# Moving the second feed-forward block's residual addition to VectorE, carrying Strassen-style sets into the last down projection, and adding ln3's beta through the output store

## The chip, the cores and the metric

The program runs on one NeuronCore of a Trainium2 chip. Its engines are TensorE (PE, matrix products), VectorE (DVE) and ScalarE (ACT) for elementwise work, GpSimd (POOL) for some elementwise work and for one kind of DMA, and SyncE (SP), which only issues DMAs here. The metric is device time of one execution in microseconds, lower is better. One execution also carries a hardware profile; its times of single instructions are what the text below quotes.

## The reference, cut to what matters

One decoder layer on 256 tokens of width 2048 in float32: a half-step feed-forward block, a mixer (windowed attention beside a convolution module), and a second half-step feed-forward block, each followed by a layer norm over alpha*x + block(x).

```python
def swiglu_ffn(x, w_gate, w_up, w_down):          # D_FF = 5632
    h = jax.nn.silu(x @ w_gate) * (x @ w_up)
    return h @ w_down
...
x = layer_norm(ALPHA * x + 0.5 * swiglu_ffn(x, ffn1...), ln1_g, ln1_b)
...                                                # mixer, then ln2
x = layer_norm(ALPHA * x + 0.5 * swiglu_ffn(x, ffn2...), ln3_g, ln3_b)
```

## The kernel before

**Products.** All large products keep float32 precision by splitting each operand into two parts, `hi` (rounded) and `lo` (the rest), and issuing three matmuls: hi*hi, hi*lo, lo*hi (`mm3`). One such product of a 128x128 block with 128x512 weights is three matmuls. For every weight tile of 128x1024, ScalarE makes `hi` by a cast and VectorE makes `lo` by a subtraction.

**Sets.** Where the two token blocks and two neighbouring k blocks meet two weight tiles, the code either issues the plain eight products (a set of kind "C", two weight sources) or a Strassen-Winograd form with seven (kind "S", four sources). An S set saves one product, three matmuls, and costs VectorE: four subtractions of 128x512 on the weights (`sub`, tiles `more` and `sum`) and more `lo` tiles, because four combinations of weights are split rather than two tiles. The token side needs sums of blocks too: `xs` for the up projections (made by `sums_of`), and extra slots of `hh` and `hl`, the split hidden activations, for the down projections.

**Parts.** A feed-forward block runs in three parts of the hidden width (16, 16 and 12 blocks of 128, `PARTS`). In a part, `pair` computes two groups of up and gate projections at a time from eight sets in the order of `UP`; the gated result is transposed (`turn`: VectorE transposes, POOL sends it through DRAM as `far` and back as `hf`), then split into `hh` and `hl` (`split`). Then the part's down projection runs. Parts 1 and 2 use `down_by_sums`: for each two of the four 512-wide column chunks, eight sets by `KINDS`; the results are added to a DRAM copy of the residual (`sides`) by accumulating DMAs. Part 3 has no kinds and uses `tokens_by`, which goes over single token blocks and column chunks, adds to the tokens in SBUF and feeds the layer norm's statistics.

**Queue of weights.** `Steps` holds the weight sources in order. Plain sources land in four `raw` tiles; the two weight tiles of an S set land in `more`, which lives in the same SBUF as the token tile `xt` (tag "xt", one buffer). So no S set can be loaded while `xt` is in use; `load` stops at the first S set until `placed` says that the place is free, and later sources wait behind it. In block two the place is free once `stored` holds all eight pieces, that is once the residual alpha*x has been scaled and written to DRAM (`residuals`, `y<-xt`). `tokens_back` takes the place back and reloads the tokens from DRAM (`xt<-y`); before, it is called in the last pair of part 3.

**Residual of block two.** `residuals(par2, 3, None, nc.vector, 1, 2)` runs beside the first token groups of block two (`token_group`: four groups of eight plain sources each). For each column chunk it loads the rows gain and beta, scales beta by alpha on ScalarE, scales the two token blocks on ScalarE, multiplies by the gain on VectorE (L592), adds beta, and stores (L611). The adding is an accumulating DMA on POOL's queue from SBUF to SBUF (L589, `xt<-rb`), and the store follows it in the same queue.

**Order.** Each engine runs its own list in order; the lists follow the order in which the Python code emits. Work is hung on coming steps by `st.at(delay, ...)`; while `st.paced` holds, `pace` puts a few VectorE jobs behind each product so that VectorE's planned backlog stays near `AHEAD`.

**End.** In `norm_to_rows` token block 0 is normalised while PE still runs the last eight half-steps of block 1 (`LAST`); gain and beta come by VectorE operations of the form (y - mean)*gain and y*r + beta (`scaled`, `last`), then plain stores on SP's queue. Block 1 follows after the last matmul.

Of the kernel before, what the change touches and what calls it, by code (L numbers as in the profile page):

```python
# [25 lines left out]
KINDS = ("SCCSCSCC", "SCCSCSCC", None)  # L26
BLOCKS = {"S": 7, "C": 4}
# [4 lines left out]
)  # L32
SUMMED = (0, 1)
# [42 lines left out]
def up_of(g, j0, plain):  # L76
    return 0 if g == plain else 2 if g == j0 // JG else 1

# [264 lines left out]
def hybrid_layer(  # L343
# [29 lines left out]
    def add_ffn(wu, wd, plain):  # L373
        for (j0, j1), kinds in zip(PARTS, KINDS):
# [94 lines left out]
    def row_chunk(r, c, name):  # L469
        t = act.tile([P, 512], F32, tag="bc", name=name, bufs=BC)  # L470
        nc.sync.dma_start(t, rows[r, c * 512 : (c + 1) * 512].partition_broadcast(P))
        return t
# [93 lines left out]
    def residuals(par, row, more, eng, start, every):  # L566
# [12 lines left out]
        for c in range(NC_):  # L579
            at = start + 1 + c * every  # L580

            def get(c=c, at=at):
# [36 lines left out]
    def norm_to_rows(b, stats, par, gb, store, kept):  # L619
# [24 lines left out]

        if b == 0:
            scaled(0)
            rsqrt(mv[:, 1:2], r, [lambda c=c: scaled(c) for c in range(1, NC_)])
        else:

            s = small.tile([P, 1], F32, tag="rs_v", name="rs_s")  # L650
            w = small.tile([P, 1], F32, tag="rs_w", name="rs_w")
            t = small.tile([P, 1], F32, tag="rs_t", name="rs_t")
            y = small.tile([P, 1], F32, tag="rs_y", name="rs_y")
            nc.scalar.activation(s, mv[:, 1:2], AF.Sqrt, bias=eps)
            nc.vector.tensor_scalar(out=w, in0=mv[:, 1:2], scalar1=EPS, scalar2=-0.5, op0=ALU.add, op1=ALU.mult)
            nc.vector.tensor_scalar(out=par[:, b, 3:4], in0=mv[:, 0:1], scalar1=-1.0, scalar2=None, op0=ALU.mult)
            nc.scalar.activation(ys[0], ys[0], AF.Identity, bias=par[:, b, 3:4])
            nc.vector.reciprocal(y, s)
            nc.gpsimd.tensor_scalar(out=t, in0=y, scalar1=y, scalar2=w, op0=ALU.mult, op1=ALU.mult)
            nc.gpsimd.tensor_scalar(out=r, in0=t, scalar1=1.5, scalar2=y, op0=ALU.add, op1=ALU.mult)  # L660
# [4 lines left out]
        if b == 0:  # L665
            for c in range(NC_):
                last(c)
        else:
# [11 lines left out]
    def block(x_, k, b):  # L680

        return x_[:, k, b * P : (b + 1) * P] if x_.shape[2] == S else x_[:, 2 * k + b]
# [117 lines left out]
    def tokens_by(lhs, k0, nk, factor, stats, finish, kept=None, lag=0):  # L800
# [7 lines left out]
        order = down_order(nk)  # L808
        skew = 0 if finish is None else SKEW if kept is None else LAST
        held, sums, halves = [], {}, []  # L810
        for n, (c, t) in enumerate(order):
            if t == 0:
                sums[c] = [psB.tile([P, 512], F32, tag="acc", name="acc0")]
                if kept is not None and c in (1, 2):
                    gu = psA.tile([P, 2, 512], F32, tag="gu", name="acc1")
                    sums[c].append(gu[:, 0])
                    halves.append(gu[:, 1, :256])
                else:
                    sums[c].append(psC.tile([P, 512], F32, tag="acc", name="acc1"))
                if kept is not None and c > 0:  # L820
# [6 lines left out]
            behind = lag if n < half - 1 else 0 if n < len(order) - skew else len(order)  # L827
# [89 lines left out]
    def down_by_sums(hh, hl, kinds, factor, side, more):  # L917

        firsts = [sum(BLOCKS[k] for k in kinds[:t]) for t in range(len(kinds))]
        places = {  # L920
            "S": ("11", "22", "12", "S1", "S2", "S3", "S4"),
# [7 lines left out]
        for c in range(0, NC_, 2):  # L929
# [6 lines left out]
            def shared(bank, tmp=tmp):  # L936
# [6 lines left out]
                add(tmp[3], bank[5], tmp[1])  # L943

            def leave(at, ps, c=c, tmp=tmp):
# [11 lines left out]
    def ffn(xc, tag, skew, begun, prepare, finish, places, back, kept=None):  # L957
        with tc.tile_pool(name=f"ffn{tag}", bufs=2) as pool:
# [4 lines left out]
            def sums_of(n):  # L963
# [10 lines left out]
                nc.vector.tensor_tensor(out=xs[:, n, 1], in0=part, in1=xs[:, n, 0].bitcast(F32), op=ALU.subtract)  # L974
# [17 lines left out]
            for part, ((j0, j1), kinds) in enumerate(zip(PARTS, KINDS)):  # L992
                n = j1 - j0
                ends = part == len(PARTS) - 1
                count = 2 * n if kinds is None else sum(BLOCKS[k] for k in kinds)
# [20 lines left out]
                def turn(g, ht, hh=hh, hl=hl, kinds=kinds):  # L1016
# [19 lines left out]
                    def split(hf, t):  # L1036
                        full = hf.rearrange("p (t k i) -> p k t i", t=4, k=8)
                        if kinds is None:
                            return parted(8 * g + 4 * t, full[:, 4 * t : 4 * t + 4])
                        kind = kinds[2 * g + t]  # L1040
                        at = sum(BLOCKS[k] for k in kinds[: 2 * g + t])
# [6 lines left out]
                        parted(at, some[:, 1:])  # L1048
                        parted(at + 3, sums)
# [3 lines left out]
                def pair(g, ups, last):  # L1053
# [7 lines left out]
                    def shared(bank):  # L1061
# [7 lines left out]
                        if last is not None:  # L1069
# [492 lines left out]
```

## Time and profile before

| | us |
|---|---|
| median of three runs | 1691.73 (1691.11 to 1694.22) |
| profiled execution | 1691.87 |
| its span on the core | 1690.1 |
| PE busy | 1666.7 |
| VectorE busy | 1392.0 |
| ScalarE busy | 925.8 |

The profiled execution is its span plus 1.8 us around it, and stands 0.14 us above the median. A page row names line, engine, operation, the tiles out<-in, the count, then busy time and the mean of one in ns, then idle time before it and what ended that. Matmul ends are modelled and overlap, so the rate of PE is read from counts over a stretch, not from the mean duration. The source lines of the three matmuls of a product are L676 to L678.

### The profile page before, as it was taken

To read this page: it belongs to the slowest core of one execution; us is meant where nothing else is said; L and a number is where in the kernel's file an instruction comes from. 1 tells how busy PE (TensorE), PEld (TensorE's weight loads), DVE (VectorE), ACT (ScalarE), POOL (GpSimd) and SP (SyncE) were. 2 spreads that over 40 slices of the span, in tenths; PEclk is the share of its full clock that TensorE was granted. 3 is DMA by queue.
4 is the path that set the end of the run, shared out by engine and by line. 5 is a ranking of instruction groups with operands and counts; after the bars stand their busy time and mean duration, and the time that the engine had idled before them with its cause. 6 is when DMAs were issued, how large, how long until landed. Compare 5 with 4: busy or idle time off the path is not lost.

```text
span 1690.1 us, 21889 instructions
## 1 busy us (share of the span) xinstructions
PE 1666.7 (99%) x7671; PEld 1383.4 (82%) x7671; DVE 1392.0 (82%) x2049; ACT 925.8 (55%) x1279; POOL 322.1 (19%) x298
## 2 busy tenths in 40 slices
PE   9999999999999999999999999799999999999997
PEld 7888888888888888888888888678888888888886
DVE  7899898888998877758887766699998888988767
ACT  6555555555555554576665564455555555555542
POOL 0100000111100010189997102000000000000100
PEclk9999999999999999999999999899999999999999
DMA  8667677677887667466654668666785666776683
GB/s 303 243 226 238 207 251 237 211 249 238 249 255 237 224 228 258 159 204 184 195 187 151 199 210 256 212 243 217 240 268 195 225 223 210 244 258 205 225 290 102
DMA packets 112239, 378.36 MB, mean 224 GB/s; under 512 B 14080, under 2 KB 14208, under 8 KB 112128
## 3 DMA queue, kind: packets, MB, share of 16 engines
q1 hardware_dynamic: 95760, 332.64, 56.7%
q0 software_dynamic: 16224, 44.05, 10.9%
q8 instruction: 60, 0.98, 0.2%
q14 instruction: 51, 0.42, 0.1%
q10 hardware_dynamic: 144, 0.26, 0.0%
HBM read 348.59 MB, written 26.21 MB: 222 GB/s over the span
## 4 chain that ended last, share of the span: by engine, by line
PE 90%; DVE 4%; DMA 4%; issue 1%; ACT 1%; POOL 0%; SPq 0%; DVEq 0%; ACTq 0%; POOLq 0%
PE sum L676 21%; PE sum L677 21%; PE sum L678 21%; PE acc L676 4%; PE acc L678 4%; PE acc L677 4%; DMA xt<-rb 2%; PE in_c L1213 2%; PE in_a L1213 2%; PE in_q L1213 1%; DVE lo L170 1%; PE grp L677 1%; PE grp L678 1%; PE grp L676 1%; PE in_a L1211 1%
## 5 line engine op out<-in xcount | busy, mean ns | idle before, releaser
L170 DVE TENSOR_TENSOR lo<-raw,hi 128x1024 fp32r<-128x1024 f32 x312 | 367.8, 1221 | 76.5 <-ACT hi L166 75.5
L676 PE MATMUL sum<-hi,xcat 128*128 128x512 f32 x1026 | 399.9, 390 | 9.3 <-DVE ht L1005 8.4
L677 PE MATMUL sum<-lo,xcat 128*128 128x512 f32 x1026 | 399.7, 390 | 1.4 <-DVE lo L170 1.4
L678 PE MATMUL sum<-hi,xcat 128*128 128x512 f32 x1026 | 399.4, 389 | 0.0
L166 ACT CAST hi<-raw 128x1024 fp32r<-128x1024 f32 x312 | 315.5, 1048 | 88.9 <-DMA raw<-in_wu 43.3
L166 ACT CAST hi<-more 128x1024 fp32r<-128x1024 f32 x186 | 168.8, 908 | 178.1 <-DVE more L184 143.4
L249 ACT CAST hi<-raw 128x1024 fp32r<-128x1024 f32 (+1 forms) x180 | 182.6, 1031 | 121.9 <-PE acc L678 57.4
L676 PEld LDWEIGHTS sum<-hi,xcat 128*128 128x128 f32 x1026 | 192.9, 188 | 50.4 <-DVE ht L1005 8.8
L677 PEld LDWEIGHTS sum<-lo,xcat 128*128 128x128 f32 x1026 | 192.9, 188 | 41.5 <-DVE lo L170 1.8
L678 PEld LDWEIGHTS sum<-hi,xcat 128*128 128x128 f32 x1026 | 192.9, 188 | 40.1
L170 DVE TENSOR_TENSOR lo<-more,hi 128x1024 fp32r<-128x1024 f32 x186 | 190.2, 1042 | 32.4 <-ACT hi L166 32.3
L252 POOL TENSOR_TENSOR lo<-raw,hi 128x1024 fp32r<-128x1024 f32 x73 | 175.5, 2424 | 114.7 <-ACT hi L249 107.7
L676 PE MATMUL sum<-hi,hh 128*128 128x512 f32 x488 | 190.1, 390 | 0.5 <-DVE part L933 0.4
L1024 POOL DMA_DIRECT2D far<-hr x88 | 49.4, 577 | 738.6 <-DVE hr L1019 738.5
L678 PE MATMUL sum<-hi,hl 128*128 128x512 f32 x488 | 189.9, 389 | 0.0
L677 PE MATMUL sum<-lo,hh 128*128 128x512 f32 x488 | 189.8, 389 | 0.0
L166 ACT CAST hi<-sum 128x512 fp32r<-128x512 f32 x124 | 77.2, 622 | 171.2 <-DVE sum L184 166.5
L252 DVE TENSOR_TENSOR lo<-raw,hi 128x1024 fp32r<-128x1024 f32 (+1 forms) x107 | 126.1, 1204 | 45.7 <-ACT hi L249 44.9
L1058 DVE TENSOR_TENSOR part<-sum,part 128x512 f32<-128x512 f32 x152 | 100.7, 687 | 23.4 <-PE sum L678 16.4
L676 PEld LDWEIGHTS sum<-hi,hh 128*128 128x128 f32 x488 | 91.6, 188 | 20.6 <-DVE part L933 1.1
L678 PEld LDWEIGHTS sum<-hi,hl 128*128 128x128 f32 x488 | 91.6, 188 | 19.1
L677 PEld LDWEIGHTS sum<-lo,hh 128*128 128x128 f32 x488 | 91.6, 188 | 18.8
(202 smaller groups left out, 2514.2 us busy)
## 6 DMA issues: line engine op xcount, KB each, us to landing
raw<-in_wu SPq DMA_DIRECT2D x272, 512.0 KB, 5.1
raw<-in_wd SPq DMA_DIRECT2D x128, 512.0 KB, 5.0
more<-in_wu SPq DMA_DIRECT2D x76, 512.0 KB, 7.0
raw<-in_win SPq DMA_DIRECT2D x52, 512.0 KB, 4.0
more<-in_wd SPq DMA_DIRECT2D x48, 512.0 KB, 7.4
raw<-in_wout SPq DMA_DIRECT2D x32, 512.0 KB, 3.7
far<-hr POOLq DMA_DIRECT2D x88, 128.0 KB, 2.7
hf<-far POOLq DMA_DIRECT2D x22, 512.0 KB, 3.7
```

Of the source, the lines that this page charges most:

```text
L166: self.nc.scalar.copy(hi, x_)
L170: self.nc.vector.tensor_tensor(out=lo, in0=x_, in1=hi.bitcast(F32), op=ALU.subtract)
L249: nc.scalar.copy(hi, raw)
L252: eng.tensor_tensor(out=lo, in0=raw, in1=hi.bitcast(F32), op=ALU.subtract)
L676: nc.tensor.matmul(ps, s_hi, m_hi, start=start, stop=False)
L677: nc.tensor.matmul(ps, s_hi, m_lo, start=False, stop=False)
L678: nc.tensor.matmul(ps, s_lo, m_hi, start=False, stop=stop)
L1024: nc.gpsimd.dma_start(far[:, :, t].rearrange("f r n -> r f n"), hr[32 * t : 32 * t + 32])
L1058: nc.vector.tensor_tensor(out=out, in0=ps, in1=other, op=ALU.add)
L1211: nc.tensor.matmul(ps[:, :S], w[1][:, n], x1[:, k, 0, :], start=False, stop=k == KT - 1)
L1213: nc.tensor.matmul(ps, w[0][:, n], x1[:, k], start=k == 0, stop=False)
```

## The change

Four things change. (1) In `residuals`, beta is added by VectorE, as an operation of 128x512 behind each gain multiplication. (2) Part 3 gets kinds, "SCCSCC". Its column chunks 0 and 1 are computed by `down_by_sums`, whose results stay in SBUF and are added to the tokens by VectorE (`joins`) at the second to fifth step of the `tokens_by` that follows for chunks 2 and 3. `tokens_back` moves from the last pair to the last S set of that down projection. In these columns an S set keeps eight blocks of `hh`/`hl` (kind "L"), since the plain products need the fourth one. (3) `UP[2]`, the order of the first pair of parts 2 and 3 in both blocks, has three S sets for two; their token sums are made in part 2's first pair. (4) At the end, block 0's beta is written to `out` ahead by a broadcast DMA from DRAM to DRAM, and its normalised rows are added by four accumulating stores on POOL's queue; ScalarE does the scaling by r and VectorE only the gain. The loads of ln3's gain and beta move from SP's queue to POOL's and ScalarE's, and from step 6 to step 1. The two last half-chunks of block 1 get PSUM tiles of their own.

```diff
-KINDS = ("SCCSCSCC", "SCCSCSCC", None)
-BLOCKS = {"S": 7, "C": 4}
+KINDS = ("SCCSCSCC", "SCCSCSCC", "SCCSCC")
+BLOCKS = {"S": 7, "C": 4, "L": 8}
 UP = (
...
-    ((0, "S"), (2, "C"), (3, "C"), (1, "S"), (4, "C"), (5, "C"), (6, "C"), (7, "C")),
+    ((0, "S"), (3, "C"), (1, "S"), (4, "C"), (5, "C"), (2, "S"), (6, "C"), (7, "C")),
 )
-SUMMED = (0, 1)
+SUMMED = (0, 1, 2)
...
-            if kinds is None:
-                sources.extend(wd[c, j0 // 4 + t // 2, t % 2] for c, t in down_order(j1 - j0))
-                continue
             for c in range(0, NC_, 2):
+                if c > 0 and j1 == JT:
+                    sources.extend(wd[c + i, t // 2, t % 2] for i in range(2) for t in range(j0 // 2, j1 // 2))
+                    continue
                 for t, kind in enumerate(kinds, j0 // 2):
...
                 def on(out, a, b_, op):
-                    if eng is nc.vector and op is ALU.add:
-                        return lambda: nc.gpsimd.dma_start(out, b_, accum_op=ALU.add)
-
                     def work():
                         eng.tensor_tensor(out=out, in0=a, in1=b_, op=op)
...
+        minus, root, w, t, y = (small.tile([P, 1], F32, tag=f"rs_{k}", name=f"rs_{k}") for k in "nvwty")
+        nc.scalar.activation(root, mv[:, 1:2], AF.Sqrt, bias=eps)
...
         if b == 0:
-            scaled(0)
-            rsqrt(mv[:, 1:2], r, [lambda c=c: scaled(c) for c in range(1, NC_)])
+            nc.gpsimd.tensor_scalar(out=minus, in0=minus, scalar1=r, scalar2=None, op0=ALU.mult)
+
+            def rest(c):
+                nc.vector.tensor_tensor(out=ys[c], in0=ys[c], in1=gb[c][0], op=ALU.mult)
+                nc.gpsimd.dma_start(out[:P, c * 512 : (c + 1) * 512], ys[c], accum_op=ALU.add)
+
+            for c in range(NC_):
+                nc.scalar.activation(ys[c], ys[c], AF.Identity, scale=r, bias=minus)
+                st.at(c + 2, lambda c=c: rest(c))
...
+        if k0 == 0:
+            order = [x_ for x_ in order if x_[0] > 1]
...
             def leave(at, ps, c=c, tmp=tmp):
 
                 t = tmp[places_[at]]
                 add(t, ps, t)
+                if columns < NC_:
+                    y = xts[0][:, 1 - at[0], (c + at[1]) * 512 : (c + at[1] + 1) * 512]
+                    joins[1 - at[0], at[1]] = lambda: nc.vector.tensor_tensor(out=y, in0=y, in1=t, op=ALU.add)
+                    return
...
                         begun()
+                        nc.gpsimd.dma_start(out[:P], rows[6].partition_broadcast(P))
                         group(1, token_group(xc, 0))
...
+                    if part == 1 and g == j0 // JG:
+                        for m in range(2, len(SUMMED)):
+                            st.at(4, lambda m=m: st.soon.append(lambda: sums_of(m)))
...
-                st.at(6, lambda: prepare(pool))
+                st.at(1, lambda: prepare(pool))
...
+                for c in range(2):
+                    for b in range(2):
+                        st.at(2 + c + 2 * b, lambda b=b, c=c: stats_of(b, c))
                 tokens_by((hh, hl), 0, n, 0.5, stats, lambda b: finish(b, stats), kept)
```

Counted over the whole program, PE issues 24 matmuls of 128x512 fewer (12 in each block), VectorE issues 16 of `lo<-raw` fewer, 24 of `lo<-more`, 16 of `lo<-sum` and 32 weight subtractions more. Three places show how the lists move.

On POOL, beside the first token groups of block two (rb is alpha*beta, y the DRAM copy, far and hf the transposed hidden block on its way through DRAM). Before:

```order
L1141 MEMSET eps 128x1
L589 DMA xt<-rb_0_9112 128x512 x2
L611 DMA y_138<-xt 128x512 x2
L589 DMA xt<-rb_1_9152 128x512
L1024 DMA far<-hr 32x4x256 x4
L1026 DMA hf<-far 128x1024
L589 DMA xt<-rb_1_9152 128x512
L611 DMA y_138<-xt 128x512 x2
L589 DMA xt<-rb_2_9195 128x512 x2
L611 DMA y_138<-xt 128x512 x2
L589 DMA xt<-rb_3_9244 128x512 x2
L611 DMA y_138<-xt 128x512 x2
```

After:

```order
L1176 MEMSET eps 128x1
L1113 DMA out<-in_rows 128x2048
L612 DMA y_138<-xt 128x512 x2
L1044 DMA far<-hr 32x4x256 x4
L1046 DMA hf<-far 128x1024
L612 DMA y_138<-xt 128x512 x6
```

The eight accumulating DMAs are gone, and the broadcast to `out` stands right behind the memset.

On VectorE, behind the last pair of part 3 in block two (hr is that pair's transposed result, hf its return from DRAM, hl the lower half of its split, raw a plain weight tile, more an S set's). Before:

```order
L1019 STREAM_TRANSPOSE hr<-ht 128x1024
L252 TENSOR_TENSOR lo_14219<-raw_14103,hi_14218 128x1024
L252 TENSOR_TENSOR lo_14225<-raw_14121,hi_14224 128x1024
L252 TENSOR_TENSOR lo_14243<-raw_14139,hi_14242 128x1024
L252 TENSOR_TENSOR lo_14261<-raw_14157,hi_14260 128x1024
L252 TENSOR_TENSOR lo_14279<-raw_14222,hi_14278 128x1024
L252 TENSOR_TENSOR lo_14299<-raw_14228,hi_14298 128x1024
L252 TENSOR_TENSOR lo_14335<-raw_14246,hi_14334 128x1024
L1033 TENSOR_TENSOR hl_13148<-hf,hh_13147 128x512 x2
```

After, the end of the same stretch:

```order
L174 TENSOR_TENSOR lo_14390<-more,hi_14389 128x1024
L174 TENSOR_TENSOR lo_14401<-more,hi_14400 128x512
L174 TENSOR_TENSOR lo_14415<-raw_14266,hi_14414 128x1024
L174 TENSOR_TENSOR lo_14429<-raw_14284,hi_14428 128x1024
L174 TENSOR_TENSOR lo_14447<-raw_14331,hi_14446 128x1024
L174 TENSOR_TENSOR lo_14462<-raw_14340,hi_14461 128x1024
L1053 TENSOR_TENSOR hl_13251<-hf,hh_13250 128x512 x2
L174 TENSOR_TENSOR lo_14487<-raw_14432,hi_14486 128x1024
L174 TENSOR_TENSOR lo_14490<-raw_14438,hi_14489 128x1024
L938 SCALAR_TENSOR_TENSOR part<-sum,part 128x512 x4
```

Seven plain `lo` stood between the transposition and hl before; now a whole S set (nine rows, of which the last two are shown) and four plain `lo` stand there, and the partial sums of the down's final S set follow.

On VectorE at the end, where token block 0 is normalised (par holds mean, variance and r, g and b are gain and beta, acc is a PSUM tile of token block 1). Before, the end of that work:

```order
L634 SCALAR_TENSOR_TENSOR xt<-xt,par_144,g_14330 128x512
L514 TENSOR_SCALAR rs_t<-par_144,rs_w 128x1
L515 TENSOR_SCALAR par_144<-rs_t,par_144 128x1
L640 SCALAR_TENSOR_TENSOR xt<-xt,par_144,b_14320 128x512
L640 SCALAR_TENSOR_TENSOR xt<-xt,par_144,b_14324 128x512
L640 SCALAR_TENSOR_TENSOR xt<-xt,par_144,b_14328 128x512
L640 SCALAR_TENSOR_TENSOR xt<-xt,par_144,b_14332 128x512
L488 SCALAR_TENSOR_TENSOR acc_14463<-acc_14463,xt 128x512
L494 BN_STATS st_14189<-acc_14463 128x6 x2
```

After, from the aggregated statistics of block 0 on:

```order
L625 BN_AGGR par_144<-st_14591 128x2
L648 TENSOR_SCALAR rs_w<-par_144 128x1
L649 TENSOR_SCALAR rs_n<-par_144 128x1
L652 RECIPROCAL rs_y<-rs_v 128x1
L659 TENSOR_TENSOR xt<-xt,g_14611 128x512
L492 SCALAR_TENSOR_TENSOR acc_14596<-acc_14596,xt 128x512
L498 BN_STATS st_14592<-acc_14596 128x6 x2
L659 TENSOR_TENSOR xt<-xt,g_14615 128x512
L659 TENSOR_TENSOR xt<-xt,g_14619 128x512
L659 TENSOR_TENSOR xt<-xt,g_14623 128x512
L492 SCALAR_TENSOR_TENSOR xt<-acc_14716,xt 128x512
```

Token block 1's next evacuation (L488, now L492) stood behind eight passes of 128x512 over block 0's tokens (four L634, of which the last is shown, and four L640); now it stands behind one (L659).

More of the change, by code (lines that the diff above doesn't have):

```diff
@@ L77, in up_of, with blocks_of @@
     return 0 if g == plain else 2 if g == j0 // JG else 1
+def blocks_of(columns):
+    return lambda kind: BLOCKS["L" if kind == "S" and columns < NC_ else kind]
 class Steps:
@@ L680, in block @@
     def block(x_, k, b):
-        return x_[:, k, b * P : (b + 1) * P] if x_.shape[2] == S else x_[:, 2 * k + b]
+        if x_.shape[2] == S:
+            return x_[:, k, b * P : (b + 1) * P]
+        kinds = KINDS[-1]
+        return x_[:, sum(4 if y == "C" else 8 for y in kinds[: k // 2]) + 2 * (k % 2) + b]
     def token_mm(ps, lhs, k0, t, nk, b, w):
@@ L813, in tokens_by @@
                 sums[c] = [psB.tile([P, 512], F32, tag="acc", name="acc0")]
[L814 to L820, printed above, removed]
+                if kept is not None and c == 2:
+                    halves.extend(psA.tile([P, 2, 512], F32, tag="gu", name="acc1")[:, 0, :256] for _ in range(2))
+                sums[c].append(psC.tile([P, 512], F32, tag="acc", name="acc1"))
+                if kept is not None:
                     kept[1, c] = [sums[c][1]] if c < NC_ - 1 else halves
@@ L826, in tokens_by @@
             held.append((c, t, w))
-            behind = lag if n < half - 1 else 0 if n < len(order) - skew else len(order)
+            behind = len(order) if n >= len(order) - skew else lag if n < half - 1 else 0
             while len(held) > behind:
@@ L915, in by_sums, with down_by_sums @@
                 st.step(0)
-    def down_by_sums(hh, hl, kinds, factor, side, more):
-        firsts = [sum(BLOCKS[k] for k in kinds[:t]) for t in range(len(kinds))]
+    joins = {}
+    def down_by_sums(hh, hl, kinds, factor, side, more, columns, last):
+        firsts = [sum(map(blocks_of(columns), kinds[:t])) for t in range(len(kinds))]
         places = {
-            "S": ("11", "22", "12", "S1", "S2", "S3", "S4"),
+            "S": ("21", "11", "22", "12", "S1", "S2", "S3", "S4")[-blocks_of(columns)("S"):],
             "C": ("21", "11", "22", "12"),
@@ L927, in blocks @@
             return hh[:, n], hl[:, n]
-        for c in range(0, NC_, 2):
+        for c in range(0, columns, 2):
             tmp, places_ = [], {(0, 0): 0, (0, 1): 2, (1, 0): 1, (1, 1): 3}
@@ L943, in shared @@
                 add(tmp[3], bank[5], tmp[1])
+                if last is not None:
+                    last()
             def leave(at, ps, c=c, tmp=tmp):
@@ L994, in ffn @@
                 ends = part == len(PARTS) - 1
-                count = 2 * n if kinds is None else sum(BLOCKS[k] for k in kinds)
+                columns = 2 if ends else NC_
+                count = sum(map(blocks_of(columns), kinds))
                 hh, hl = (pool.tile([P, count, P], F32R, tag=t, name=f"{t}{part}", bufs=1) for t in ("hh", "hl"))
@@ L1014, in group, with turn @@
                         turn(g // 2, gated.pop())
-                def turn(g, ht, hh=hh, hl=hl, kinds=kinds):
+                def turn(g, ht, hh=hh, hl=hl, kinds=kinds, ends=ends, of=blocks_of(columns)):
                     hr = pool.tile([P, 4, 2 * P], F32, tag="ht", name="hr")
@@ L1047, in split, with pair @@
                         block_sums(view, [some[:, k] for k in range(4)])
-                        parted(at, some[:, 1:])
-                        parted(at + 3, sums)
+                        n = of(kind) - 4
+                        parted(at, some[:, 4 - n :])
+                        parted(at + n, sums)
                     st.at(6, lambda: st.soon.extend([lambda t=t: split(hf, t) for t in range(2)]))
-                def pair(g, ups, last):
+                def pair(g, ups):
                     tmp, places = [], {(0, 0): 0, (0, 1): 2, (1, 0): 1, (1, 1): 3}
```

69 lines of the change are left out of this document (36 added, 33 removed).

## The prediction

> **What bounds the kernel now.** I read the page first, then PE's busy time in 50 us stretches, then what PE waited for, then the chain of waits.
>
> ```profile
> PE 1666.7 (99%) x7671; PEld 1383.4 (82%) x7671; DVE 1392.0 (82%) x2049; ACT 925.8 (55%) x1279; POOL 322.1 (19%) x298
> ...
> 1000.00:1050.00 50.00, 50.00 (x222) 41.43 (x221) 32.80 (x47) 26.57 (x36) 10.48 (x15) 1.00 0.84 265
> 1050.00:1100.00 50.00, 40.20 (x164) 32.32 (x163) 30.40 (x40) 20.58 (x27) 6.90 (x11) 0.90 0.65 216
> ...
> 1200.00:1600.00 400.00, 400.00 (x1766) 331.31 (x1766) 347.75 (x438) 214.74 (x267) 30.19 (x47) 1.00 0.69 230
> ...
> PE sum L676 <- DVE ht L1005: 8.4, 1, 8.4
> PE sum L677 <- DVE lo L170: 1.4, 1, 1.4
> ...
> PE acc L676 <- DVE st L494: 0.8, 1, 0.8
> ```
>
> In the stretches, the columns after the length are busy time and count of PE, weight loads, VectorE, ScalarE, POOL, then PE's granted clock, the DMA share and GB/s. PE is the bound: it is busy without a break nearly everywhere, at 400/1766 = 0.2265 us per matmul in the long steady stretch, which is the price of a matmul below. One stretch is different: from 1050 to 1100 PE issues 164 matmuls where its neighbour has 222, and the clock drops. The two longest waits of PE lie there. The chain of waits (start, length, what) says why:
>
> ```profile
> 1009.62 9.78 DMA xt<-rb
> ...
> 1033.07 7.75 DMA xt<-rb
> 1041.79 8.28 DMA xt<-rb
> ...
> 1054.27 4.30 DMA xt<-rb
> 1058.97 2.35 DMA y<-xt
> 1061.78 4.36 DMA more<-in_wu
> 1066.23 0.70 DVE sum L184
> ...
> POOL y L611 <- DMA xt<-rb: 27.2, 7, 6.9
> ```
>
> The residual's beta is added by accumulating DMAs, whose landings follow each other in the chain; each store waits for them on POOL's queue (27.2 us in seven waits), and only when the last store has landed, at 1061.3, may the first S set's weights (`more`) be loaded. VectorE gets them at 1066.2. The releaser named for the 8.4 us, ht, is only VectorE work queued behind that set.
>
> What the whole disturbance costs is read between two fixed points, the first matmul of block two's first pair and that of part 2's first pair:
>
> ```profile
> 1052.81 0.39 PE L676 MATMUL sum<-hi,xcat 128*128 128x512 f32 x1
> ...
> 1235.40 0.39 PE L676 MATMUL sum<-hi,xcat 128*128 128x512 f32 x1
> ```
>
> Between them lie two pairs of 2 S and 6 C sets (2*7 + 6*8 = 62 products) and two down passes of 3 S and 5 C (61 products), so 246 products or 738 matmuls, 167.2 us at 0.2265. It took 182.6. The loss is **15.4 us**: 9.8 in the two waits, the rest in a slow clock and in shorter gaps behind.
>
> ```profile
> 1070.00:1075.00 5.00, 2.76 (x7) 2.18 (x8) 4.29 (x6) 1.70 (x5) 0.79 (x2) 0.50 0.74 302
> 1075.00:1080.00 5.00, 5.00 (x16) 3.95 (x15) 4.61 (x6) 3.77 (x6) 1.99 (x4) 0.66 0.76 189
> ```
>
> Of the 7.76 us that PE was busy here, 23 matmuls are worth 5.2 at full rate, so the clock cost 2.6. [...]
>
> **The change part by part.**
>
> *Beta by VectorE.* This takes eight accumulating DMAs out of POOL's queue and puts eight additions on VectorE.
>
> ```profile
> L592 DVE TENSOR_TENSOR xt<-xt,rg 128x512 f32<-128x512 f32 x8 | 5.5, 688 | 7.3 <-ACT xt L602 7.3
> ...
> 1028.75 0.69 DVE L592 TENSOR_TENSOR xt<-xt,rg 128x512 f32<-128x512 f32 x1
> ...
> 1054.03 1.23 DVE L252 TENSOR_TENSOR lo<-raw,hi 128x1024 fp32r<-128x1024 f32 x1 [0.68 <-ACT hi L249]
> ...
> 1019.88 25.30 SPq L110 DMA_DIRECT2D raw<-in_wu  x9
> ...
> more<-in_wu SPq DMA_DIRECT2D x76, 512.0 KB, 7.0
> ...
> y<-xt POOLq DMA_DIRECT2D x8, 256.0 KB, 4.3
> ```
>
> The last gain multiplication ends at 1029.4. With eight additions of 0.69, 5.5 us at most, the last piece is ready by 1035, and with 0.6 to issue and 4.3 to land the place is free by 1040. SP comes to the S set's request only behind the nine plain requests, at 1045.2, so the place is no longer what is late; the weights land at 1052.2, and VectorE reaches them behind its last plain `lo`, at 1055.3. PE needs the set behind two C sets, 48 matmuls after 1052.81: at 1063.7. An S set is some 7.2 us of VectorE work (below), its first tile ready after three or four of them, so there are about 5 us to spare. The additions themselves lie beside PE work on a VectorE that is busy 32.8 of 50 us; without that cover they would cost 5.5. I take the whole 15.4; the bounds are 15.4 and, if half of it stays, 7.7. The broadcast of beta to `out`, 1 MB, has no row of its own kind; it is issued behind the memset, before the residual's stores, and no one waits for it before the end. I take nothing; had it to move like four of the 256 KB stores at 4.3 us one after another, it would load the DMA engines for 17 us, against a prefetch several tiles ahead.
>
> *Fewer products.* Parts 2 and 3 of both blocks start with a third S set: four products. Part 3's down has two S sets, once per block for the two columns: four products. 8*3 = 24 matmuls at 0.2265 are **5.4 us**, if PE stays the bound. That depends on VectorE:
>
> ```profile
> L170 DVE TENSOR_TENSOR lo<-more,hi 128x1024 fp32r<-128x1024 f32 x186 | 190.2, 1042 | 32.4 <-ACT hi L166 32.3
> ...
> L170 DVE TENSOR_TENSOR lo<-raw,hi 128x1024 fp32r<-128x1024 f32 x312 | 367.8, 1221 | 76.5 <-ACT hi L166 75.5
> ...
> L170 DVE TENSOR_TENSOR lo<-sum,hi 128x512 fp32r<-128x512 f32 x124 | 80.2, 688 | 0.0
> ...
> L184 DVE TENSOR_TENSOR sum<-more,sum 128x512 f32<-128x512 f32 x62 | 42.9, 692 | 2.1
> ...
> L184 DVE TENSOR_TENSOR sum<-more 128x512 f32<-128x512 f32 x62 | 41.9, 676 | 13.1 <-DMA more<-in_wu 11.2 <-DMA more<-in_wd 1.7
> ...
> 1021.20 0.68 DVE L969 TENSOR_TENSOR full<-xcat 128x512 f32<-128x512 f32 x1
> ...
> 1023.63 0.69 DVE L974 TENSOR_TENSOR xs<-sums,xs 128x512 fp32r<-128x512 f32 x1 [0.69 <-ACT xs L973]
> ...
> 1446.80:1488.00 41.20, 41.20 (x184) 34.12 (x183) 38.41 (x49) 23.00 (x28) 4.48 (x6) 1.00 0.74 232
> ...
> 1238.00:1280.00 42.00, 42.00 (x187) 34.80 (x186) 33.47 (x39) 20.42 (x26) 1.51 (x2) 1.00 0.77 245
> 1488.00:1530.00 42.00, 42.00 (x187) 34.80 (x186) 33.71 (x40) 19.80 (x24) 2.19 (x3) 1.00 0.77 248
> ```
>
> An S set costs VectorE three `lo` from `more` (3.13), two from `sum` (1.38) and four subtractions between 0.68 and 0.69 (2.74): 7.2 us. A C set costs 2*1.22 = 2.4. A third S set adds 4.8. The two first pairs (last two rows) have 33.5 and 33.7 us of VectorE work in 42; part 3's becomes 38.5 in 41.2, which a down pass of 3 S sets carries today without a gap (38.4 in 41.2). Part 2's also gets the third token sums, 2.4 us of work (3.1 with its wait, 1021.20 to 1024.32): 40.9 in 41.2. That is fuller than any stretch here. VectorE runs several weight tiles ahead of PE, so a few tenths are absorbed; below nothing is excluded.
>
> *Part 3's down pass* puts S sets where the split of the last pair must come in time. In the down pass of part 2 the same sequence reads:
>
> ```profile
> 1404.24 1.29 DVE L1058 TENSOR_TENSOR part<-sum,part 128x512 f32<-128x512 f32 x2 [1.89 <-PE sum L678]
> ...
> 1424.50 1.29 DVE L1033 TENSOR_TENSOR hl<-hf,hh 128x512 fp32r<-128x512 f32 x2
> ```
>
> From PE's end of the pair to that split are 20.3 us. In part 3 the first four kinds, S C C S, keep PE for 30 products, 20.4 us, and the split is needed then; today the order there leaves room. Two of the S operations that stand ahead of it in part 2 are plain `lo` now, about as long. So it arrives as it is needed, with 0 to 2 us of waiting in each block. Together with part 2's full pair I put **1.4 us** of new waits against the saving (0.7 per block; bounds 0 and about 6). The joins, eight additions and their statistics, replace evacuations of the same columns beside PE work.
>
> *The end.*
>
> ```profile
> 1669.56 0.26 DVE L624 BATCH_NORM_AGGREGATE par<-st 128x2 f32<-128x24 f32 x1
> ...
> 1676.90 0.69 DVE L488 SCALAR_TENSOR_TENSOR acc<-acc,xt 128x512 f32<-128x512 f32 x1
> ...
> DMA to landing us min/median/max: 5.3/7.6/10.4
> ```
>
> Block 1's evacuation stands behind 7.3 us of block 0's normalisation. Behind one gain pass it comes while PE still works, so PE's wait of 0.8 (the last tile pair has its own PSUM now) and a little behind it go: **1.0 us**. The accumulating stores cost what the last row shows for such DMAs into DRAM (line L951): up to 10.4. The last is ready about 8 us after 1669.6, so it lands by 1688, when the plain last store does too. Nothing lost, or a few tenths.
>
> The sum against the profiled execution: 1691.87 - 15.4 - 5.4 - 1.0 + 1.4 = **1671.5** us, and 0.14 less against the median, which I ignore.
>
> **The rivals.**
>
> *VectorE becomes the bound.* If in part 2's and 3's first pairs and in the short down pass VectorE's work and its waits on ScalarE no longer fit, the eight products bring nothing, and part 2's pairs may even lengthen by the token sums, up to 2.4 in each block. For it speaks 40.9 of 41.2; against it, that 38.4 of 41.2 runs without a gap. Time: 1691.87 - 15.4 - 1.0 = 1675.5, up to 1680.3.
>
> *The stall stays in part.* The place is free, but the weights behind nine plain requests, or VectorE with 5.5 us more in its list, are late. For it: ScalarE and VectorE already wait on the rows of gain and beta (7.3 in L592's row). Against: 5 us to spare, and the accumulating traffic is gone. Half of 15.4 left: 1679.
>
> *The accumulating stores end the kernel.* If the four run one after another from 1674 on at 10.4 each, the last lands at 1715.6 where the span now ends at 1690.1, and the time is 1671.5 + 1 + 25.5 = 1698, slower than before; from about 9 us each it loses. In the chain the SBUF additions did follow each other. Against: L951's stores come in groups of four and none took longer than 10.4, so they overlap, and the DMA engines are nearly idle at the end.
>
> **How the numbers follow.** The forecast gets 0.70 with a range of its own of 1668 to 1675, the first rival 0.17, the second 0.10, the third 0.03. The range 1667.5 to 1681 takes in the first two rivals. A change of 0.2%, 3.4 us, is about what can be told from none. All but the third lie far below it: faster 0.96, within 0.01, slower 0.03.
>
> **What would show it right or wrong.** In the changed profile: no wait of PE above 2 us near 1060 and a granted clock of 1.00 there; `more` requested near 1045; 1766 matmuls in 400 us as before; VectorE above 40 of 41 us in part 2's first pair with PE unbroken; a PE wait on hl of under 2 us in the short down pass; the last landing a plain store. A wait of several us in any of these places, or an `out` accumulate landing last, would make it wrong.

## The result, and the profile after

The changed kernel takes **1674.91 us** (median of 4 runs, 1672.95 to 1675.41) against 1692.15 (4 runs, 1691.11 to 1694.22): a ratio of 0.9894, with a 95% interval of 0.9877 to 0.9912. That is 17.2 us faster. The forecast was 1671.5, 3.4 us too low; the range of 1667.5 to 1681 holds the time. The first rival's 1675.5 is nearer to it than the forecast, so the time alone does not tell the two apart, and the traces have to. The profiled execution took 1675.41 us, its span 1673.6.

The first group below is the page's busy time; the second is PE's busy time by stretches (length, then busy time and count of PE, weight loads, VectorE, ScalarE and POOL, then granted clock, DMA share, GB/s); the third is all that PE waited for.

```profile
PE 1657.9 (99%) x7647; PEld 1375.4 (82%) x7647; DVE 1444.1 (86%) x2151; ACT 944.6 (56%) x1316; POOL 323.0 (19%) x302
```

```profile
258.70:299.90 41.20, 41.20 (x183) 34.13 (x182) 38.84 (x51) 22.20 (x28) 2.19 (x4) 1.00 0.70 235
1050.00:1100.00 50.00, 49.44 (x217) 40.28 (x216) 41.49 (x55) 25.88 (x36) 2.80 (x5) 1.00 0.59 213
1200.00:1600.00 400.00, 400.00 (x1766) 331.20 (x1766) 362.58 (x470) 222.00 (x281) 27.19 (x42) 1.00 0.67 225
1219.99:1261.20 41.21, 41.21 (x183) 34.15 (x182) 39.52 (x53) 22.47 (x29) 2.93 (x4) 1.00 0.72 230
```

```profile
PE idle L415 <- DVE ones L412: 1.2, 1, 1.2
PE acc L678 <- DVE lo L256: 1.1, 2, 0.9
PE sum L677 <- DVE part L938: 1.0, 2, 0.9
PE grp L780 <- ACT hi L253: 0.5, 1, 0.5
PE sum L677 <- DVE part L1077: 0.4, 1, 0.4
```

The stretch from 1050 to 1100, which held 164 matmuls at a clock of 0.90, now holds 217 at 1.00. The waits of 8.4 and 1.4 us are gone; none is above 0.9 any more, apart from the start. 24 matmuls fewer are executed (7647 for 7671), and they still run at 1766 in 400 us. VectorE is at 38.8 and 39.5 of 41.2 us in the first pair of part 2 (first and last row of the stretches), in the two blocks, and PE has no gap there.

Where the time went is best read between fixed points of PE's instructions. The stretches are those of the prediction, in us; the second column of "after" is the changed kernel run once more. "Last form" is the version found below, with the PSUM bank and the spread joins (two runs).

| stretch | before | after | after, again | last form |
|---|---|---|---|---|
| block one, part 2's down | 83.93 | 85.71 | 84.85 | 84.66, 84.27 |
| block one, part 3's down | 67.28 | 65.71 | 65.80 | 65.70, 65.70 |
| block two, first sum to part 2's first sum | 182.59 | 168.43 | 168.29 | 168.60, 167.49 |
| pairs of part 2, each block | 168.64 | 167.96 | 167.96 | 167.96, 167.96 |
| pairs of part 3, each block | 126.48 | 125.80 | 125.80 | 125.80, 125.80 (126.01 once, in block one) |
| block two, part 3's down to the last matmul | 66.37 | 65.62 | 66.02 | 63.95, 63.95 |
| last matmul's start to the span's end | 10.24 | 11.27 | 11.25 | 10.43, 10.65 |

From before to after that is +1.8, -1.6, -14.2, four times -0.7, -0.75 and +1.0, which is 16.4 of the 16.5 us between the two profiled executions. Two rows got longer, and the prediction had neither lengthening: a down pass of block one, and the end.

The end, on VectorE and POOL (start, length, instruction, idle time before it and its releaser). Before:

```profile
1681.91 1.40 DVE L634 SCALAR_TENSOR_TENSOR acc<-acc,par,g 128x512 f32<-128x512 f32 x2
1682.11 0.34 POOL L659 TENSOR_SCALAR rs_t<-rs_y,rs_w 128x1 f32<-128x1 f32 x1 [52.28 <-DVE rs_y L658]
1682.79 1.26 POOL L662 TENSOR_TENSOR xt<-xt,g 128x512 f32<-128x512 f32 x1
1683.22 1.40 DVE L640 SCALAR_TENSOR_TENSOR xt<-acc,par,b 128x512 f32<-128x512 f32 x2
```

After:

```profile
1664.39 0.73 DVE L635 SCALAR_TENSOR_TENSOR xt<-xt,par,g 128x512 f32<-128x512 f32 x1
1664.58 0.76 POOL L653 TENSOR_SCALAR rs_t<-rs_y,rs_w 128x1 f32<-128x1 f32 x1 [1.59 <-DVE rs_y L652]
1665.67 1.26 POOL L667 TENSOR_TENSOR xt<-xt,g 128x512 f32<-128x512 f32 x1
1665.74 1.73 DVE L641 SCALAR_TENSOR_TENSOR xt<-xt,par,b 128x512 f32<-128x512 f32 x1
1667.39 0.74 DVE L641 SCALAR_TENSOR_TENSOR xt<-acc,par,b 128x512 f32<-128x512 f32 x1
```

The same work is longer in two places. POOL's one-column step takes 0.76 us instead of 0.34, and VectorE's first multiply-add takes 1.73, where its neighbour takes 0.74. Both overlap an instruction of the other engine. What is new is where column 1 of token block 1 lies: its name is `acc` (PSUM) before and `xt` (SBUF) after, because a join now produces it.

### The profile page after: what moved, and what is told of

It reads as the page before. It is cut to its first block, busy times and chain, and to the rows that moved or that the text cites. A ratio compares the mean times of both kernels' runs of the same rounds, so it can differ in the third digit from the quotient of the medians.

```text
span 1673.6 us, 21985 instructions
## 1 busy us (share of the span) xinstructions
PE 1657.9 (99%) x7647; PEld 1375.4 (82%) x7647; DVE 1444.1 (86%) x2151; ACT 944.6 (56%) x1316; POOL 323.0 (19%) x302
## 5 line engine op out<-in xcount | busy, mean ns | idle before, releaser
L170 ACT CAST hi<-more 128x1024 fp32r<-128x1024 f32 (+1 forms) x210 | 190.6, 907 | 178.8 <-DVE more L188 158.7
L174 DVE TENSOR_TENSOR lo<-more,hi 128x1024 fp32r<-128x1024 f32 (+1 forms) x210 | 213.7, 1040 | 20.3 <-ACT hi L170 20.2
L677 PE MATMUL sum<-hi,hh 128*128 128x512 f32 x580 | 226.2, 390 | 1.3 <-DVE part L938 1.0
L678 PE MATMUL sum<-lo,hh 128*128 128x512 f32 x580 | 225.7, 389 | 0.0
L679 PE MATMUL sum<-hi,hl 128*128 128x512 f32 x580 | 225.7, 389 | 0.0
L253 ACT CAST hi<-raw 128x1024 fp32r<-128x1024 f32 (+1 forms) x156 | 158.5, 1029 | 93.2 <-PE acc L679 42.2
L677 PEld LDWEIGHTS sum<-hi,hh 128*128 128x128 f32 x580 | 108.8, 188 | 25.8 <-ACT hi L170 1.3
L679 PEld LDWEIGHTS sum<-hi,hl 128*128 128x128 f32 x580 | 108.9, 188 | 22.7
L678 PEld LDWEIGHTS sum<-lo,hh 128*128 128x128 f32 x580 | 108.9, 188 | 22.6 <-DVE lo L174 0.2
L256 DVE TENSOR_TENSOR lo<-raw,hi 128x1024 fp32r<-128x1024 f32 (+1 forms) x83 | 97.7, 1198 | 25.7 <-ACT hi L253 25.5
```

The costliest lines, as they stand in the source:

```text
L170: self.nc.scalar.copy(hi, x_)
L174: self.nc.vector.tensor_tensor(out=lo, in0=x_, in1=hi.bitcast(F32), op=ALU.subtract)
L253: nc.scalar.copy(hi, raw)
L256: eng.tensor_tensor(out=lo, in0=raw, in1=hi.bitcast(F32), op=ALU.subtract)
L677: nc.tensor.matmul(ps, s_hi, m_hi, start=start, stop=False)
L678: nc.tensor.matmul(ps, s_hi, m_lo, start=False, stop=False)
```

## Experiments

**Beta alone.** The kernel before, with one edit:

```diff
                 def on(out, a, b_, op):
-                    if eng is nc.vector and op is ALU.add:
-                        return lambda: nc.gpsimd.dma_start(out, b_, accum_op=ALU.add)
-
                     def work():
```

> The kernel before with one edit of the change: beta of FFN2's residual is added by VectorE, not by accumulating DMAs. Theory (those DMAs are the whole cause of the stall): 14.2 to 15.4 us less, 1676.8 to 1678.0, with 167.2 to 168.4 us from the first sum of block two to the first of part 2, and no PE wait over 1.2 us there. Rival (part of the stall stays, behind the plain requests or VectorE's list, and other parts of the change took it away): 1680 or more, the part 171 us or longer.

Measured: 1677.43 us (1676.63 to 1678.66), ratio 0.9918, interval 0.9905 to 0.9932. Block two's part 1 takes 168.60 us. The accumulating DMAs were the cause of the stall: without them 14.0 of its 15.4 us are gone, by this edit alone. The waits of PE say where the other 1.4 lie:

```profile
PE sum L673 <- DVE part L930: 1.0, 2, 0.9
PE acc L673 <- DVE st L494: 0.8, 1, 0.8
PE sum L673 <- DVE part L1055: 0.6, 1, 0.6
```

L1055 is VectorE's read-out of a pair's PSUM banks: at 1099 us the second pair needs a bank while VectorE is still behind. The first row lies in block one's part 2's down, where this program is the kernel before word for word; there it took 83.93 us in the one execution and 84.57 in the other. So a difference of 0.6 us in that pass can be chance.

**The third S set on top of it.** To the run above:

```diff
-    ((0, "S"), (2, "C"), (3, "C"), (1, "S"), (4, "C"), (5, "C"), (6, "C"), (7, "C")),
+    ((0, "S"), (3, "C"), (1, "S"), (4, "C"), (5, "C"), (2, "S"), (6, "C"), (7, "C")),
 )
-SUMMED = (0, 1)
+SUMMED = (0, 1, 2)
...
+                    if part == 1 and g == j0 // JG:
+                        for m in range(2, len(SUMMED)):
+                            st.at(4, lambda m=m: st.soon.append(lambda: sums_of(m)))
...
```

> The run before this one plus the third S set in the first pair of parts 2 and 3 of both blocks: four products, 12 matmuls, less. Theory (PE stays the bound): 2.7 us less than beta alone. If the fuller first pair of part 2 is what leaves VectorE late in the down pass behind it (1.8 us more than before in block one), 1.0 to 1.3 less only. Rival (VectorE is the bound): no less than beta alone, or more.

Measured: 1675.35 us (1674.48 to 1676.24), ratio 0.9906, interval 0.9891 to 0.9921: 2.1 us less than beta alone. In the trace the pairs of parts 2 and 3 are each 0.68 us shorter, to the hundredth what three matmuls cost, in both blocks: four times 0.68 is 2.7. PE is the bound there and VectorE is not. Block one's part 2's down is 85.24, 0.7 above the run before. That is too little to read a cost of the fuller pair from it: up to this pass the code of block one is the same in nine of the runs here (the changed kernel twice, its last form twice, the old end, the PSUM bank, the joins spread, POOL's passes left out, beta by POOL), and they have 84.27 to 85.97.

**The old end.** The changed kernel, with block 0 of the last norm as before:

```diff
         if b == 0:
...
-            for c in range(NC_):
-                nc.scalar.activation(ys[c], ys[c], AF.Identity, scale=r, bias=minus)
-                st.at(c + 2, lambda c=c: rest(c))
+            scaled(0)
+            rsqrt(mv[:, 1:2], r, [lambda c=c: scaled(c) for c in range(1, NC_)])
...
+            for c in range(NC_):
+                last(c)
...
-                        nc.gpsimd.dma_start(out[:P], rows[6].partition_broadcast(P))
```

> The changed kernel with block 0's normalisation and stores as before: eight passes on VectorE, plain stores, no broadcast of beta to the output. Theory of the prediction (the new end takes PE's wait of 0.8 and a little more): 1.0 us slower than the changed kernel, 1675.9, with a PE wait of about 0.8 at the last half. Rival (the new end is worth nothing, the accumulating stores and POOL cost what is won): 1674.9 or less. If the long multiply-add of block 1 (1.73 us) is still there, the accumulating stores are not its cause.

Measured: 1674.34 us (1671.92 to 1676.50), ratio 0.9901, interval 0.9885 to 0.9916. It is no slower than the changed kernel. Two points follow. First, PE has no wait at the last half here either; the one wait left in that down pass is 0.8 on `lo`. So the wait of 0.8 did not go because of the new order of the end. Before, PE waited there for the statistics of the column that shared a PSUM tile with the second half, and in the changed kernel each half has a tile of its own. That this is what took the wait away is argued from the trace; no run sets these tiles apart from the rest of the change. What the new order brings is that block 1's statistics are complete 1.24 us after the last matmul's start instead of 1.98, and the end takes 11.25 us instead of 11.75. The last down pass in front of it took 65.09 us with the old end and 65.62 and 66.02 with the new one, so in the sum nothing is left that these runs can show. Second, the long multiply-add is still there without any accumulating store:

```profile
1663.36 0.75 POOL L660 TENSOR_SCALAR rs_t<-rs_y,rs_w 128x1 f32<-128x1 f32 x1 [18.70 <-DVE rs_y L659]
1664.51 1.73 DVE L641 SCALAR_TENSOR_TENSOR xt<-xt,par,b 128x512 f32<-128x512 f32 x1
```

**Column 1 in PSUM.** The bank beside one of the two half tiles is free. The join of block 1's column 1 writes there:

```diff
-                    halves.extend(psA.tile([P, 2, 512], F32, tag="gu", name="acc1")[:, 0, :256] for _ in range(2))
+                    gus = [psA.tile([P, 2, 512], F32, tag="gu", name="acc1") for _ in range(2)]
+                    halves.extend(gu[:, 0, :256] for gu in gus)
+                    kept[1, 1] = [gus[0][:, 1]]
...
```

> The changed kernel, but the join of block 1's column 1 writes into a free PSUM bank instead of the token tile, so that VectorE's two last passes over this column read one operand from PSUM, as they did in the kernel before. Theory (VectorE with two SBUF operands and POOL hold each other up at the end): the multiply-add falls from 1.73 to 0.7 us, POOL's first step from 0.76 to 0.34, and the time by 1.0 to 1.4 us, to 1673.5 to 1673.9. Rival (POOL is late because it has just issued the accumulating stores, or the tail is longer for another reason): 1674.9, within 0.3, with the tail still 11.3.

Measured: 1674.37 us (1673.71 to 1677.41) beside 1675.03 (1672.83 to 1676.48) for the changed kernel on the same chip, ratios 0.9908 (0.9887 to 0.9930) and 0.9905 (0.9887 to 0.9923). The times can't tell these apart, and the 1.0 us expected does not show in them. The traces can:

```profile
1663.58 1.40 DVE L635 SCALAR_TENSOR_TENSOR acc<-acc,par,g 128x512 f32<-128x512 f32 x2
1663.78 0.33 POOL L653 TENSOR_SCALAR rs_t<-rs_y,rs_w 128x1 f32<-128x1 f32 x1 [1.64 <-DVE rs_y L652]
1664.89 1.40 DVE L641 SCALAR_TENSOR_TENSOR xt<-acc,par,b 128x512 f32<-128x512 f32 x2
```

The multiply-add is back at 0.7, POOL's step at 0.33, and the span ends 10.38 us after the last matmul's start (11.25 beside it).

**POOL's two passes left out.** The changed kernel without the multiplication by the gain and the addition of beta for column 0 of block 1, so that the two are missing from that piece of the output:

```diff
-            nc.gpsimd.tensor_tensor(out=ys[0], in0=ys[0], in1=gb[0][0], op=ALU.mult)
             nc.scalar.mul(ys[0], ys[0], r)
-            nc.gpsimd.tensor_tensor(out=ys[0], in0=ys[0], in1=gb[0][1], op=ALU.add)
```

> The changed kernel without POOL's two passes over block 1's column 0, which leaves gain and beta of that piece out of the output. Theory (VectorE's multiply-add with two SBUF operands stands still while POOL works on SBUF): it takes 0.75 us instead of 1.73, and the time falls by 1.0 to 1673.9. Rival (it is long for another reason, a late r or a slow operand): it stays at 1.7, the time within 0.3 of 1674.9.

Measured: 1673.83 us (1672.60 to 1674.13), ratio 0.9895, interval 0.9880 to 0.9910; the end takes 10.11 us.

```profile
1664.00 0.73 DVE L635 SCALAR_TENSOR_TENSOR xt<-xt,par,g 128x512 f32<-128x512 f32 x1
1664.19 0.75 POOL L653 TENSOR_SCALAR rs_t<-rs_y,rs_w 128x1 f32<-128x1 f32 x1 [1.63 <-DVE rs_y L652]
1665.34 0.75 DVE L641 SCALAR_TENSOR_TENSOR xt<-xt,par,b 128x512 f32<-128x512 f32 x1
```

VectorE's instruction, with the same operands and the same place in its list, takes 0.75 us when POOL has no pass at that time. POOL's step, which still meets VectorE's pass over two SBUF operands, still takes 0.75. So the cause of the longer end is shown from both sides: by moving VectorE's operand to PSUM, and by taking POOL's passes away.

**Joins spread.** The changed kernel, with the joins at every second step:

```diff
-                        st.at(2 + c + 2 * b, lambda b=b, c=c: stats_of(b, c))
+                        st.at(2 + 2 * (c + 2 * b), lambda b=b, c=c: stats_of(b, c))
```

> The changed kernel, but the four joins of the last down pass come at steps 2, 4, 6, 8 instead of 2, 3, 4, 5. Theory (four joins and statistics in a row, 1.4 us each, make VectorE's lower halves of the weights late): the two waits of PE for lo, 1.4 us in block two, go, and the time falls by 1.4 to 1673.5. Rival (the weights themselves land late, behind 2 MB of tokens and 1 MB of rows): the waits stay, 1674.9. A third: the later joins hold up the loads of the gain rows and block 0's normalisation, 1675.5 or more.

Measured: 1673.17 us (1671.84 to 1674.16), ratio 0.9895, interval 0.9878 to 0.9912, 1.9 below the changed kernel beside it, though the two ranges overlap. Block two's part 3's down takes 63.95 us instead of 66.02, and both waits of PE for `lo` are gone from its list:

```profile
PE idle L415 <- DVE ones L412: 1.2, 1, 1.2
PE sum L677 <- DVE part L938: 1.0, 2, 0.9
PE sum L677 <- DVE part L1077: 0.9, 1, 0.9
PE grp L780 <- ACT hi L253: 0.2, 1, 0.2
```

How that looks on VectorE, first in the changed kernel, then with the joins spread:

```profile
1644.97 0.68 DVE L958 TENSOR_TENSOR xt<-xt,part 128x512 f32<-128x512 f32 x1
1645.69 0.75 DVE L1142 BATCH_NORM_STATS2 st<-xt 128x6 f32<-128x256 f32 x2
1646.36 1.21 DVE L256 TENSOR_TENSOR lo<-raw,hi 128x1024 fp32r<-128x1024 f32 x1
1647.48 0.68 DVE L958 TENSOR_TENSOR xt<-xt,part 128x512 f32<-128x512 f32 x1
1648.20 0.75 DVE L1142 BATCH_NORM_STATS2 st<-xt 128x6 f32<-128x256 f32 x2
1648.87 1.21 DVE L256 TENSOR_TENSOR lo<-raw,hi 128x1024 fp32r<-128x1024 f32 x1
```

```profile
1642.85 0.68 DVE L958 TENSOR_TENSOR xt<-xt,part 128x512 f32<-128x512 f32 x1
1643.57 0.69 DVE L1142 BATCH_NORM_STATS2 st<-xt 128x6 f32<-128x512 f32 x1
1644.18 2.34 DVE L256 TENSOR_TENSOR lo<-raw,hi 128x1024 fp32r<-128x1024 f32 x2
```

A join with its statistics ahead of every `lo` puts the last two of them at 1646.4 and 1648.9, when PE is already there; spread, the same two are done by 1646.5 (this run stands 1.0 us earlier when the pass begins). The third theory has a small share: the end takes 11.51 us here for 11.25, as block 1's last statistics come 0.24 us later.

**Both.** The PSUM bank and the spread joins together:

> Both edits, the PSUM bank and the spread joins. If both theories hold and the gains add: 1674.9 - 1.0 - 1.4 = 1672.5 us. If neither: 1674.9.

> The version with the PSUM bank and the spread joins once more, as the measure for the three beside it: 1673.1 us; in block one some 84.7 us from the first product of part 2's down to the first of part 3 (82.9 without a wait), in block two 168.6 us from its first sum to part 2's (167.2 without a wait).

Measured: 1673.09 us (1671.90 to 1673.85), ratio 0.9894, interval 0.9877 to 0.9911, on the chip where the changed kernel took 1675.03; and 1672.05 (1670.37 to 1676.14), ratio 0.9885, interval 0.9869 to 0.9902, on another. That is 2 to 3 us below the changed kernel's medians. The intervals overlap, so the times alone do not prove it. The traces put 1.7 to 2.1 us of it into the last down pass and 0.6 to 0.8 into the end, in both runs. By its medians it is the fastest version run here.

**The residual's pieces earlier.** On that version, an edit for block one's down pass. Around the place where PE waits there (415 to 475 us in the changed kernel) the weights land later than in the same 60 us of block two, and five transfers of block one's residual lie beside them. The transfers of the sets' weights (count, size, median us to landing), block one's first:

```profile
more<-in_wd SPq DMA_DIRECT2D x8, 512.0 KB, 9.4
```

```profile
more<-in_wd SPq DMA_DIRECT2D x10, 512.0 KB, 7.4
```

The edit moves the pieces of the residual to earlier steps:

```diff
-            st.at(96 + 8 * n, one, True)
+            st.at(96 + 6 * n, one, True)
```

> The same with the eight pieces of block one's residual six steps apart instead of eight, so that none of them moves while part 2's down runs. Theory (these pieces slow the weights' landing there, 9.4 us against 7.4 for a set in block two, and so VectorE and PE): the down falls from 84.7 to 83.0 us and the time by 1.7 to 1671.4. Rival (VectorE is simply full there): still 84.7; or the wait moves into the pairs of part 2, now 167.96 us without a break.

Measured: 1675.50 us (1673.18 to 1680.77), ratio 0.9907, interval 0.9890 to 0.9923. The edit did move the pieces out (a last one is being stored as the pass begins), and the weights landed sooner, in the same 60 us:

```profile
more<-in_wd SPq DMA_DIRECT2D x8, 512.0 KB, 6.6
```

So the first half of the theory holds (9.3 in the last form without the edit). The second fell: weights that land sooner did not take PE's wait away. The down takes 86.56 us, and the pairs of part 2, in which more of the pieces lie now, take 169.63 instead of 167.96. Since PE already waits for VectorE in those pairs here, the run does not fully clear the weights as a cause. The row below holds one wait in those pairs, one behind them and one in block two:

```profile
PE sum L677 <- DVE part L1079: 2.7, 3, 1.2
```

What makes this down pass lose 1 to 3 us in block one (3.6 in this run), and nothing in block two, where it takes 82.96 us in every run, stays open. The wait is VectorE's read-out of a bank, and it is there before the change too (1.0 us of loss in the one execution of the kernel before, 1.6 in the run with beta alone, 2.8 in the changed kernel).

**Beta by POOL.** On the same version:

```diff
+                    on_ = nc.gpsimd if eng is nc.vector and op is ALU.add else eng
+
                     def work():
-                        eng.tensor_tensor(out=out, in0=a, in1=b_, op=op)
-                        if eng is nc.vector:
+                        on_.tensor_tensor(out=out, in0=a, in1=b_, op=op)
+                        if on_ is nc.vector:
```

> The version of the first run with beta of block two's residual added by POOL instead of VectorE: 5.5 us less on VectorE, some 10 us on POOL. Theory (VectorE's lateness behind the residual makes PE wait, and POOL is free): 168.6 falls to 167.2 to 167.6, the time by 1.0 to 1672.1. Rival (VectorE's additions and subtractions of SBUF operands and POOL's stand in each other's way, as at the end): VectorE's plain lo there rise from 1.22 us towards 2.5, the part stays at 168.6 or grows, the time 1673.1 or more.

> Both edits on the version of the first run. If both theories hold, 1673.1 - 1.7 - 1.0 = 1670.4 us; if neither, 1673.1.

Measured with beta by POOL: 1675.83 us (1675.14 to 1676.32), ratio 0.9904, interval 0.9890 to 0.9917, against 1672.05 beside it; with the earlier pieces 1679.94 (1679.02 to 1682.82), ratio 0.9930, interval 0.9916 to 0.9944. Neither edit gains: they cost 3.5 (the pieces) and 3.8 us (POOL), and 7.9 together. Block two's part 1 takes 171.15 us with POOL, 167.49 without. VectorE's groups from 1010 to 1100 us, first without and then with POOL's additions (count, busy, mean ns), and behind them a row of each engine's timeline with POOL's additions:

```profile
L593 DVE TENSOR_TENSOR xt<-xt,rg 128x512 f32<-128x512 f32 x5 | 3.4, 688 | 0.0
L1003 DVE TENSOR_TENSOR sums<-full,sums 128x128 f32<-128x128 f32 x2 | 0.6, 293 | 0.1
```

```profile
L595 DVE TENSOR_TENSOR xt<-xt,rg 128x512 f32<-128x512 f32 x5 | 5.6, 1123 | 0.0
L1005 DVE TENSOR_TENSOR sums<-full,sums 128x128 f32<-128x128 f32 x2 | 3.4, 1722 | 0.1
...
1030.06 3.15 DVE L1005 TENSOR_TENSOR sums<-full,sums 128x128 f32<-128x128 f32 x1
1030.50 2.54 POOL L595 TENSOR_TENSOR xt<-xt,rb 128x512 f32<-128x512 f32 x2
```

An operation on small sums that takes 0.29 us took 3.15 while two additions of POOL ran, and ended only behind both. The rival had the right mechanism, and most of the victims were others: the multiplications by the gain and the small sums paid. One plain `lo` did:

```profile
1003.94 1.29 POOL L595 TENSOR_TENSOR xt<-xt,rb 128x512 f32<-128x512 f32 x1 [37.75 <-DVE xt L595]
1004.10 2.21 DVE L256 TENSOR_TENSOR lo<-raw,hi 128x1024 fp32r<-128x1024 f32 x1 [0.25 <-ACT hi L253]
1006.84 1.21 DVE L256 TENSOR_TENSOR lo<-raw,hi 128x1024 fp32r<-128x1024 f32 x1
1006.99 2.21 POOL L595 TENSOR_TENSOR xt<-xt,rb 128x512 f32<-128x512 f32 x1 [1.77 <-DVE xt L595]
```

In the first two rows POOL began first, and VectorE's 1.22 became 2.21; in the last two VectorE began first, and POOL's 1.29 became 2.21. What less work on VectorE would bring without this meeting was not run.

## Why the prediction was right, and where it was off

- **The stall.** Right in cause and place, and the largest term. In the changed kernel:

```profile
1041.82 0.80 SPq L159 DMA_DIRECT2D more<-in_wu  x2
1050.54 0.69 DVE L188 TENSOR_TENSOR sum<-more 128x512 f32<-128x512 f32 x1 [2.13 <-DMA more<-in_wu]
```

`more` is requested at 1041.8 (the prediction had 1045.2), and VectorE begins on it at 1050.5 (1055.3). The granted clock is 1.00 from 1050 to 1100 us (0.90 before), and 1.00 in both of the prediction's stretches from 1070 to 1080 (0.50 and 0.66 before). The step "I take the whole 15.4" was 1.2 us too high: the run with beta alone gives 14.0 in this stretch, the change 14.2. In place of the stall stands a wait for the read-out of a bank (0.4 us named in the changed kernel, 0.6 with beta alone), because VectorE is still behind when the first pair ends. It varies: against 167.2 the stretch loses 0.1 us in the run with beta and the third S set, 1.4 with beta alone and 1.8 with the joins spread, so 13.6 to 15.3 of the 15.4 came, from run to run.
- **The products.** Right in the pairs, to a hundredth. The rival in which VectorE becomes the bound is refuted there by the four pairs at exactly -0.68 and by VectorE at 38.8 to 39.5 of 41.2 with PE unbroken. The prediction had 40.9, and took it from part 3's pair; from the row of part 2's own, 33.5, it is 40.7. In block two's short down pass the rival was right in part: there PE waited for VectorE, and the waits took all of the 1.4 us of the two products saved.
- **New waits, 1.4 us.** The sum was too small, and its cause was another one. No wait of PE on hl appears. PE waited for two plain `lo` behind the joins in block two (1.1 and 1.5 us named, 1.7 to 2.1 in the stretch), work of which the prediction only says that it would "replace evacuations of the same columns beside PE work". With the joins spread these waits are gone, so this is shown. Block one's part 2's down, where nothing was expected, took 0.9 to 1.8 us more than in the profile before. The same code takes 84.27 to 85.97 us there, from run to run, and the cause of the loss was not found, so this part is open.
- **The end, 1.0 us.** Here the step failed. PE's wait of 0.8 did go, and not by the new order of block 0's work, which the prediction put first: it is gone with the old order too. What is left for it is the PSUM tiles of the two halves, which the prediction had in brackets. The new order shortens the end by 0.5 us, which no sum of these runs shows. Against it stands 1.0 us that no step had: column 1 of block 1, which the joins moved from PSUM to SBUF, makes VectorE and POOL stand in each other's way (1.73 us for a multiply-add that takes 0.75 without POOL's pass). The prediction followed the joins' cost on VectorE, and not where their results lie for the steps behind them.
- **The accumulating stores.** Right: nothing waits for them. They landed in at most 5.5 us, the last was issued at 1662.1, and a plain store lands last. The broadcast to `out` landed in 6.0 us. Block two's part 1, beside which it runs, takes 167.3 to 168.6 us in three runs without it and 167.5 to 169.0 in seven with it (those with the edits of the last two experiments aside), so a cost of it does not show.

Between the two profiled executions the change brought 16.5 us where the sum had 20.4. By the stretches of the table, measured less predicted: the stall +1.2; the end behind the last matmul +1.2 (+1.0 for -0.2); block two's last down pass +0.7 (-0.75 for two products, the wait of 0.8 and half of the new waits, -1.46); block one's -0.9 (-1.57 for -0.66); block one's part 2's down +1.8; the pairs nothing. That is the 4 us. So the mechanism of the two large terms was right, and the miss is the small ones. That the forecast's own 1668 to 1675 still holds 1674.91 is luck by 0.1 us.

## What to carry to other kernels

When a result moves from PSUM to SBUF, look at which later VectorE passes then read two SBUF operands, and whether POOL works at that moment; at the end of this program one such meeting made a pass of 0.75 us 1.73 long and the end 1.0 us longer. VectorE's busy share can fit and PE can still wait where VectorE's list bunches: in the changed kernel VectorE was busy for 51.7 of the 66.0 us of the last down pass, but for 9.5 of the ten from 1640 to 1650, and PE was busy for only 9.1 of those. Spread small jobs over the steps of the loop, and count the waits in the stretch. Moving work from VectorE (busy for 39.3 of the 50 us from 1000 to 1050 in the changed kernel) to POOL (7.2) was no relief with operands in SBUF: 5.5 us less for VectorE made this kernel 3.8 us slower.

## What the hardware showed that was not expected

In the rows shown above, where a VectorE instruction that reads two SBUF operands overlapped a POOL instruction that reads SBUF, one of the two ended only behind the other. It shows as a longer duration, not as idle time: 0.75 became 1.73 us for a 128x512 multiply-add, 0.34 became 0.76 for a POOL step on one column, 1.22 became 2.21 for a plain `lo`, 1.29 became 2.21 for an addition of POOL's, and 0.29 became 3.15 behind two POOL additions. With one of VectorE's operands in PSUM the multiply-add and POOL's step are back at 0.70 and 0.33.
